# Two trunk layers on one core: the opening stage without GpSimd, its loads reordered, and some low parts in the FFNs issued earlier

## The chip, the core and the metric

The kernel runs on one core of a Trainium2 chip. A core has TensorE (PE, matrix products), VectorE (DVE), ScalarE (ACT), GpSimd (POOL) and SyncE (SP), which here issues every DMA. The time is device microseconds (us) of one execution. The kernel before took a median of 1766.38 us in 3 runs (1763.32 to 1766.62).

## The reference

Two layers of a diffusion trunk work on 384 tokens (256 latent, 128 context) of width 1024. Per layer there are three sub-layers, each with its own modulation by a condition vector (one for latent, one for context tokens):

```
m = silu(cond) @ w_mod[l] + b_mod[l]             # 9 vectors of 1024: shift, scale, gate for 3 sub-layers
mod(x, i) = x * (1 + m[3i+1]) + m[3i]
h = (silu(mod(x,0) @ w1) * (mod(x,0) @ w3)) @ w2         # FFN, inner width 2816
x = LN(alpha * x + 0.5 * m[2] * h)
x = LN(alpha * x + m[5] * Mix(mod(x, 1)))                # three token mixers, gates, output projection
h = second FFN on mod(x, 2);  x = LN(alpha * x + 0.5 * m[8] * h)
```

All matrices are float32. So the kernel runs four FFNs and two mixers, and before the first product of the first FFN it needs the shift and scale of that sub-layer: 2048 columns of w_mod, 16 units of 128 columns, each times two conditions.

## The kernel before, in words

**Split products.** Each large product is made of three float32r products: a factor is split into a high part (its float32r rounding) and a low part (the rest), and hi*hi, hi*lo and lo*hi are added in PSUM (`mm3`). A unit of weights is a 128x1024 tile, 512 KB, loaded by SP (`raw`); ACT makes its high part (`whi`, L263) and DVE its low part (`wlo`, L268). `pump` splits units as long as fewer than ten are held, `take` hands the next one to PE, and `done` frees it.

**GEMVs.** All other modulation units (128 of them) are made while the FFNs and mixers run: a tile `wm` of w_mod is loaded, and DVE multiplies it with silu(cond), which stands broadcast on all partitions in `silu_bc`, and sums along the row: two passes per unit, one for each condition (`gemv_acc`, L312). In an FFN `tick` calls `pump` and then lets GEMVs run at a steady pace: `GEMV_TICKS` is the number of ticks over which the FFN's share (`FFN_GEMV`: 42 in the first) is spread. In the first FFN there are 52 ticks.

**FFN.** Chunk j is 128 of the 2816 inner columns. For it PE makes w1 and w3 products (PSUM tiles named `f`, 24 products of 128x384 each), ACT makes silu (`s`), DVE the product `h`, ACT its high part `hhi`, DVE its low part `hlo`. The low part is a function kept in the list `lows` and called after the next `tick`. One chunk later PE multiplies `hhi`, `hlo` with a unit of w2 into `acc`. The last six units of w2 are the `tail`: PE takes them one output tile after another, so that the last chunk's `hlo` is needed a few us after its `h`. In FFNs other than the first, chunks 0 and 1 are made first for latent tokens, then for context tokens in another layout (`f1c`, `hc`), which `ctx_h` transposes into place at chunk 2.

**Opening stage** (`start`). It loads x, the conditions, the 16 modulation units (`m`) and the first ten weight units (`w`), transposes x (`xr` to `xl`, `xc`), makes the modulation columns `AB`, applies them (`y`), splits the result into `xT_hi` and `xT_lo` for eight 128-row blocks of the model width, and runs the first four chunks of FFN 1 (PSUM tiles named `st`, 192 products). The modulation units are shared out: those in `ON_PE` are GEMVs on PE (two moving columns), those in `ON_POOL` are multiplied on POOL and summed on ACT, the others go to DVE. The conditions come as one row each, are split, spread over the partitions by eight matmuls against ones (`sb`), and run through silu. Five of ten `wlo`, and the four `hlo`, are made on POOL. The order on every engine comes from a list scheduler (`Jobs.emit`), which takes each job's planned duration and dependences; loads keep the order of `START_LOADS`. It counts PSUM banks ("B") as a stock, and not the 34 SBUF tiles ("Q") of 4 KB per partition in which all weights live.

Of the kernel before, what the change touches and what calls it, by code (L numbers as in the profile page):

```python
# [11 lines left out]
F32 = mybir.dt.float32  # L12
# [6 lines left out]
P = 128  # L19
# [23 lines left out]
N_PE0 = 16  # L43
ON_PE = (0, 3, 7, 8, 10)
ON_POOL = (5, 9, 15)
LO_ON_V = (0, 1, 4, 5, 9)
AFTER = 2
START_LOADS = [('m', 0), ('m', 2), ('x', 2), ('b', 0), ('m', 9), ('x', 5), ('w', 0), ('x', 4), ('x', 0), ('m', 8),
               ('w', 1), ('m', 10), ('x', 3), ('w', 2), ('m', 1), ('m', 3), ('w', 3), ('m', 11), ('w', 4), ('x', 1),
               ('m', 12), ('m', 5), ('w', 5), ('m', 4), ('w', 6), ('m', 7), ('m', 14), ('w', 7), ('m', 6), ('w', 8),  # L50
               ('m', 13), ('w', 9), ('m', 15)]
LATENCY = 0.18, 1.8
# [8 lines left out]
RES_AT = 5  # L61
GEMV_TICKS = 52
FFN_GEMV = {(0, 0): 42, (0, 1): 36, (1, 0): 36, (1, 1): 8}
# [117 lines left out]
def trunk_kernel(ctx: ExitStack, tc: tile.TileContext, wst, wmod, wmod0, x_lat, x_ctx, cvec, cT,  # L181
# [408 lines left out]
    def ffn(l, f, ctx_part, gate_at):  # L590
# [22 lines left out]
        else:  # L613
# [30 lines left out]
            rel(*bb)  # L644
            rel(sg)
            tick()

# [12 lines left out]
        for j in range(j0, NF):  # L660
            bb = []
            for w in ("w1", "w3"):
                i, hi, lo = take(w, l, f, j)
                b = get("B", [P, T], F32, "f1")
                for kc in range(KC):
                    mm3(b, (hi[:, kc * P:(kc + 1) * P], lo[:, kc * P:(kc + 1) * P]), xt(kc, 0, T), kc == 0, kc == KC - 1)
                done(i)
                bb.append(b)
                if w == "w3":
                    new_h(j)  # L670
                    lows.append(glu(bb[0], bb[1], T, *hT[j]))
                    rel(*bb)
                tick()
                while lows:
                    lows.pop(0)()
                if j == 2 and w == "w1":
                    ctx_h()
            if not first and j == RES_AT:
# [663 lines left out]
    with tc.manual_schedule():  # L1342
        def start(new_h, hT):
# [5 lines left out]
            sT = cst.tile([P, KC, 2], F32, name="sT")  # L1349
            ones = get("S", [1, P], F32R, "ones")  # L1350
            V.memset(ones.bitcast(F32), 1.0)
            box = {}


            def load(key, src, t=None, dur=1.46):
                def f():
                    box[key] = get("Q", [P, 1024], F32, "ld") if t is None else t
                    nc.sync.dma_start(box[key], src)
                return add("D", dur, [], f)

            def load_raw():
                return add("D", 1.46, [], issue_dma)

            crow = [get("Q", [1, 2, 512], F32, "crow") for _ in range(2)]
            ld = {"cT": load("cT", cT, cTs, .3)}
            for cd in range(2):
                ld["c", cd] = load(("c", cd), cvec[cd:cd + 1, :], crow[cd], .2)
            ld["id"] = load("id", cident, ident, .2)
            for kind, n in START_LOADS:
                if kind == "m":  # L1370
                    ld["m", n] = load(("m", n), wmod0[n])
                elif kind == "w":
                    ld["w", n] = load_raw()
                elif kind == "x":
# [4 lines left out]
                    ld["x", n] = load(("x", n), src[:, sl], xa[ti][:, sl], .73)  # L1379
# [5 lines left out]
            spread = []  # L1385
            for cd in range(2):
                hi, lo = get("Q", [1, 2, 512], F32R, "chi"), get("Q", [1, 2, 512], F32R, "clo")
                jh = add("A", .95, [ld["c", cd]], lambda hi=hi, cd=cd: S.copy(hi, crow[cd]))
                jl = add("V", 1.14, [jh], lambda hi=hi, lo=lo, cd=cd:
                         V.tensor_tensor(lo, crow[cd], hi.bitcast(F32), ALU.subtract))  # L1390

                def bc(cd=cd, parts=(hi, lo)):
                    for h in range(2):
                        b = get("B", [P, 512], F32, "sb")
                        for e in range(2):
                            mm(b, ones, parts[e][:, h, :], e == 0, e == 1)
                        box["sb", cd, h] = b
                    rel(crow[cd], *parts)
                jm = add("P", 1.7, [jl], bc, need=["B", "B"])
                for h in range(2):  # L1400
                    def ev(cd=cd, h=h):
                        b = box["sb", cd, h]
                        S.activation(sbc[:, cd, h * 512:(h + 1) * 512], b, AF.Silu)
                        rel(b)
                    spread.append(add("A", .5, [jm], ev, free=["B"]))

# [4 lines left out]
            for ti in range(3):  # L1411
                for h in range(2):
# [9 lines left out]
                    xev[ti, h] = add("A", .5, [add("P", .8, [ld["x", 2 * ti + h], ld["id"]], tr, need=["B"])], ev, free=["B"])  # L1422

# [15 lines left out]
            for kc in range(KC):  # L1439
                deps = []  # L1440
                for u in (KC + kc, kc):
                    col = modcol[0][:, u // KC, :, kc]
                    if u in ON_PE:
                        def f(u=u):
# [4 lines left out]
                            rel(box["m", u])  # L1449
                        deps.append(add("P", 1.8, [ld["m", u], silu_cols], f))  # L1450
                    else:
                        pool = u in ON_POOL
                        for cd in range(2):
                            if pool:
                                def f(u=u, cd=cd):
                                    w = box["m", u]
                                    t = box["mt", u, cd] = get("Q", [P, 1024], F32, "wms") if cd == 0 else w
                                    G.tensor_tensor(t, w, sbc[:, cd, :], ALU.mult)

                                def f2(u=u, cd=cd):  # L1460
                                    S.activation(junk, box["mt", u, cd], AF.Copy,
                                                 accum_out=modcol[0][:, u // KC, cd, u % KC:u % KC + 1])
                                    rel(box["mt", u, cd])
                                d = add("G", 2.3, [ld["m", u]] + spread + deps[-1:] * cd, f)
                                deps.append(add("A", 1.1, [d], f2))
                            else:
                                def f(u=u, cd=cd):
                                    gemv_acc(0, u, box["m", u], (cd,))
                                    if cd:
                                        rel(box["m", u])  # L1470
                                deps.append(add("V", 1.16, [ld["m", u]] + spread + deps[-1:] * cd, f))
# [5 lines left out]
                jab = add("V", .26, deps + [ld["b"]], f)  # L1477

# [11 lines left out]
                jy = add("A", .9, [jab] + [xev[ti, kc // 4] for ti in range(3)], fy)  # L1490
                lo_x.append(add("V", .5, [add("A", .45, [jy], fhi)], flo))

# [3 lines left out]
            for i in range(n_un + AFTER):  # L1496
                jh = add("A", .95, [ld["w", i]] + lo_w[-1:], split_hi)
                eng = "V" if i in LO_ON_V else "G"
                lo_w.append(add(eng, 2.3 if eng == "G" else 1.14, [jh], lambda e=eng: split_lo(G if e == "G" else V)))
            count = {}  # L1500
# [10 lines left out]
            for g in range(n_un):  # L1511
                last[g] = []
                for kc in range(KC):
                    last[g].append(add("P", .49, [lo_x[kc], lo_w[g]] + ([last[g - 1][kc]] if g else []) + last[g][:1],
                                       lambda g=g, kc=kc: prod(g, kc), need=["B"] if kc == 0 and g < 6 else []))
            for j in range(N_ST):
# [12 lines left out]
                def f4(j=j):  # L1529
                    G.tensor_tensor(hT[j][1], box["h", j], hT[j][0].bitcast(F32), ALU.subtract)  # L1530
                    rel(box["s", j], box["h", j])
                d = add("A", .4, last[2 * j], f1)
                d = add("V", .5, [d] + last[2 * j + 1], f2)
                d = add("A", .45, [d], f3)
                add("G", 1., [d], f4)
            jobs.emit({"B": 6})
            rel(ones, *xl, xc, box["wide"], *[box["st", g] for g in range(6)])
            for dst, src in ((lncol, lnT), (pscale, pscaleT), (subln, sublnT), (namask_t, namask)):
# [125 lines left out]
```

## Time and profile before

| What | Value |
|---|---|
| median of 3 runs | 1766.38 us |
| profiled execution, its span | 1768.49 us, 1766.8 us |
| PE busy | 1726.4 us, 98% of the span |
| DVE, ACT, POOL busy | 1245.9, 751.3, 37.4 us |
| mean granted clock of PE | 0.992 |
| the chain that ended last | PE 91%, DVE 4%, DMA 2% |

The profile is one execution. PE is on the chain nearly always, so time is to be looked for where PE waits, or where its clock is at the lower of its two levels (1.2 GHz, shown as 0.5, against 2.4 GHz, shown as 1.0). A table of waits names for each engine what it waited for, the total, the number of times and the longest. A window row shows busy time per engine in a stretch, the granted clock, the share of DMA time and GB/s.

### The profile page before, as it was taken

To read this page: it belongs to the slowest core of one execution; us is meant where nothing else is said; L and a number is where in the kernel's file an instruction comes from. 1 tells how busy PE (TensorE), PEld (TensorE's weight loads), DVE (VectorE), ACT (ScalarE), POOL (GpSimd) and SP (SyncE) were. 2 spreads that over 40 slices of the span, in tenths; PEclk is the share of its full clock that TensorE was granted. 3 is DMA by queue.
4 is the path that set the end of the run, shared out by engine and by line. 5 is a ranking of instruction groups with operands and counts; after the bars stand their busy time and mean duration, and the time that the engine had idled before them with its cause. 6 is when DMAs were issued, how large, how long until landed. Compare 5 with 4: busy or idle time off the path is not lost.

```text
span 1766.8 us, 24383 instructions
## 1 busy us (share of the span) xinstructions
PE 1726.4 (98%) x9444; PEld 1621.3 (92%) x9444; DVE 1245.9 (71%) x2045; ACT 751.3 (43%) x1322; POOL 37.4 (2%) x21
## 2 busy tenths in 40 slices
PE   7899998999999999999999999999999999999997
PEld 7799998899999989999998999988999999999996
DVE  6698888568785788787677788764778657755334
ACT  5433333358653452323353232334875445333321
POOL 3400000000000000000000000000000000000000
PEclk9899999999999999999999999999999999999999
DMA  8386665142446256566436666523223543644320
GB/s 319 120 291 228 238 222 196 72 169 75 138 155 226 96 207 231 206 235 223 151 122 235 224 217 229 203 88 133 106 104 117 191 143 104 237 169 141 137 96 36
DMA packets 88071, 301.64 MB, mean 171 GB/s; under 512 B 11058, under 2 KB 13970, under 8 KB 87956
## 3 DMA queue, kind: packets, MB, share of 16 engines
q1 hardware_dynamic: 87956, 300.09, 47.9%
q8 instruction: 74, 1.21, 0.3%
q14 instruction: 41, 0.34, 0.1%
HBM read 296.86 MB, written 3.19 MB: 170 GB/s over the span
## 4 chain that ended last, share of the span: by engine, by line
PE 91%; DVE 4%; DMA 2%; ACT 1%; issue 1%; SPq 0%; DVEq 0%; ACTq 0%
PE f L220 36%; PE acc L220 24%; PE gt L220 11%; PE v L220 4%; PE pj L220 4%; DVE junk L312 2%; PE qb L220 2%; PE kb L220 2%; PE o L220 1%; PE ss L220 1%; PE st L220 1%; PE f1c L220 1%; PE qc L220 1%; PE kc L220 1%; DMA wm<-in_wmod 1%
## 5 line engine op out<-in xcount | busy, mean ns | idle before, releaser
L268 DVE TENSOR_TENSOR wlo<-raw,whi 128x1024 fp32r<-128x1024 f32 x379 | 456.8, 1222 | 166.7 <-ACT whi L263 166.0
L220 PE MATMUL f<-xT_hi,whi 128*128 128x384 f32 (+1 forms) x1344 | 445.3, 331 | 0.0
L220 PE MATMUL f<-xT_hi,wlo 128*128 128x384 f32 (+1 forms) x1344 | 444.9, 331 | 0.0
L220 PE MATMUL f<-xT_lo,whi 128*128 128x384 f32 (+1 forms) x1344 | 444.6, 331 | 0.0
L263 ACT CAST whi<-raw 128x1024 fp32r<-128x1024 f32 x384 | 384.8, 1047 | 23.3 <-DMA raw<-in_wst 11.7
L312 DVE CUSTOM_DVE_ANT_0 junk<-wm,silu_bc 128x1024 bf16<-128x1024 f32 x256 | 312.5, 1221 | 6.8 <-DMA wm<-in_wmod 2.5
L220 PE MATMUL acc<-whi,hlo 128*128 128x512 f32 x624 | 246.7, 395 | 8.6 <-DVE hlo L586 8.5
L220 PEld LDWEIGHTS f<-xT_hi,whi 128*128 128x128 f32 x1344 | 252.7, 188 | 2.4
L220 PEld LDWEIGHTS f<-xT_lo,whi 128*128 128x128 f32 x1344 | 252.7, 188 | 2.4
L220 PEld LDWEIGHTS f<-xT_hi,wlo 128*128 128x128 f32 x1344 | 252.6, 188 | 0.0
L220 PE MATMUL acc<-whi,hhi 128*128 128x512 f32 x624 | 245.7, 394 | 0.9 <-ACT hhi L582 0.9
L220 PE MATMUL acc<-wlo,hhi 128*128 128x512 f32 x624 | 245.6, 394 | 0.0
L582 ACT CAST hhi<-h 128x384 fp32r<-128x384 f32 (+1 forms) x84 | 42.5, 506 | 360.0 <-DVE h L581 360.0
L220 PEld LDWEIGHTS acc<-whi,hlo 128*128 128x128 f32 x624 | 118.1, 189 | 35.5 <-DVE hlo L586 10.7
L579 ACT ACTIVATE s<-f 128x384 f32<-128x384 f32 (+1 forms) x84 | 40.7, 484 | 242.9 <-PE f L220 242.9
L581 DVE TENSOR_TENSOR h<-s,f 128x384 f32<-128x384 f32 (+1 forms) x84 | 45.5, 542 | 137.3 <-PE f L220 128.3
L220 PEld LDWEIGHTS acc<-whi,hhi 128*128 128x128 f32 x624 | 118.4, 190 | 24.4 <-ACT hhi L582 1.4
L220 PEld LDWEIGHTS acc<-wlo,hhi 128*128 128x128 f32 x624 | 118.1, 189 | 23.2
L220 PE MATMUL gt<-xT_hi,whi 128*128 128x384 f32 x384 | 130.2, 339 | 0.6 <-ACT whi L263 0.6
L220 PE MATMUL gt<-xT_hi,wlo 128*128 128x384 f32 x384 | 129.3, 337 | 1.4 <-DVE wlo L268 1.4
L220 PE MATMUL gt<-xT_lo,whi 128*128 128x384 f32 x384 | 129.2, 336 | 0.0
L220 PEld LDWEIGHTS gt<-xT_hi,wlo 128*128 128x128 f32 x384 | 72.7, 189 | 2.0 <-DVE wlo L268 2.0
(230 smaller groups left out, 2127.6 us busy)
## 6 DMA issues: line engine op xcount, KB each, us to landing
raw<-in_wst SPq DMA_DIRECT2D x384, 512.0 KB, 4.2
wm<-in_wmod SPq DMA_DIRECT2D x128, 512.0 KB, 4.6
ld<-in_wmod SPq DMA_DIRECT2D x16, 512.0 KB, 9.5
gate<-gd SPq DMA_DIRECT2D x12, 512.0 KB, 4.1
lng<-in_lnrow SPq DMA_DIRECT2D x6, 512.0 KB, 3.8
lnb<-in_lnrow SPq DMA_DIRECT2D x6, 512.0 KB, 5.1
nab<-in_nabias SPq DMA_DIRECT2D x4, 512.0 KB, 6.0
out<-y SPq DMA_DIRECT2D x6, 256.0 KB, 2.0
```

Of the source, the lines that this page charges most:

```text
L220: PE.matmul(out, a, b, start=start, stop=stop)
L263: S.copy(ws[i][0], raws[i])
L268: eng.tensor_tensor(ws[i][1], raw, ws[i][0].bitcast(F32), ALU.subtract)
L312: V.tensor_tensor_reduce(out=junk, in0=t, in1=silu_bc["t"][:, cd, :], scale=1.0, scalar=0.0, op0=ALU.mult, op1=ALU.add, accum_out=modcol[l ...
L579: S.activation(s, b1, AF.Silu)
L581: V.tensor_tensor(h, s, b3, ALU.mult)
L582: S.copy(hT_hi, h)
```

## The change

In the opening stage POOL has no work any more: the units of `ON_POOL`, the five `wlo` and the four `hlo` go to DVE, and the set of units on PE is another one, with six units for five. The two conditions are loaded broadcast to all partitions (512 KB each) straight into `silu_bc`, where ACT applies silu in place; the split, the matmuls against ones and their evacuations are gone. The loads stand in another order. The scheduler's durations are changed and it counts the "Q" tiles as a stock. In the FFNs the first two chunks' low parts are issued before the first `tick`, `ctx_h` before the `tick` of its place, and in the last chunk no GEMV is issued between `h` and `hlo`, and `pump` comes after them; `GEMV_TICKS` is 48 for 52.

```
-ON_PE = (0, 3, 7, 8, 10)
-ON_POOL = (5, 9, 15)
-LO_ON_V = (0, 1, 4, 5, 9)
+ON_PE = (1, 5, 7, 12, 13, 15)
-START_LOADS = [('m', 0), ('m', 2), ('x', 2), ('b', 0), ('m', 9), ('x', 5), ('w', 0), ('x', 4), ('x', 0), ('m', 8),
...
+START_LOADS = [('x', 2), ('x', 0), ('m', 0), ('m', 1), ('m', 9), ('m', 12), ('m', 8), ('x', 3), ('m', 7), ('b', 0),
+               ('m', 6), ('m', 10), ('x', 4), ('m', 15), ('x', 5), ('m', 2), ('m', 5), ('w', 0), ('w', 1), ('x', 1),
...
-GEMV_TICKS = 52
+GEMV_TICKS = 48
@@ ffn, after the context part of chunks 0 and 1
             rel(sg)
+            while lows:
+                lows.pop(0)()
             tick()
@@ ffn, in the loop over chunks
                     lows.append(glu(bb[0], bb[1], T, *hT[j]))
                     rel(*bb)
-                tick()
+                if j == 2 and w == "w1":
+                    ctx_h()
+                if j < NF - 1:
+                    tick()
                 while lows:
                     lows.pop(0)()
-                if j == 2 and w == "w1":
-                    ctx_h()
+                if j == NF - 1:
+                    pump()
@@ start
-            crow = [get("Q", [1, 2, 512], F32, "crow") for _ in range(2)]
-            ld = {"cT": load("cT", cT, cTs, .3)}
+            ld = {"cT": load("cT", cT, cTs, .1)}
             for cd in range(2):
-                ld["c", cd] = load(("c", cd), cvec[cd:cd + 1, :], crow[cd], .2)
+                ld["c", cd] = load(("c", cd), cvec[cd:cd + 1, :].to_broadcast([P, DM]), sbc[:, cd, :], 1.3)
...
+            spread = [add("A", 1.15, [ld["c", cd]], lambda cd=cd: S.activation(sbc[:, cd, :], sbc[:, cd, :], AF.Silu))
+                      for cd in range(2)]
...
-                        deps.append(add("P", 1.8, [ld["m", u], silu_cols], f))
+                        deps.append(add("P", 3.15, [ld["m", u], silu_cols], f, free="Q"))
...
-                eng = "V" if i in LO_ON_V else "G"
-                lo_w.append(add(eng, 2.3 if eng == "G" else 1.14, [jh], lambda e=eng: split_lo(G if e == "G" else V)))
+                lo_w.append(add("V", 1.25, [jh], lambda: split_lo(V), free="Q"))
...
-                    G.tensor_tensor(hT[j][1], box["h", j], hT[j][0].bitcast(F32), ALU.subtract)
+                    V.tensor_tensor(hT[j][1], box["h", j], hT[j][0].bitcast(F32), ALU.subtract)
...
-            jobs.emit({"B": 6})
+            jobs.emit({"B": 6, "Q": len(free["Q"])})
```

On PE, at the start of the opening stage, before (the rows with sT are GEMV units, sb the broadcast, xr transposes of x, xT_hi the first wide products):

```order
L220 MATMUL st_116<-sT,ld_107 128x2 x8
L220 MATMUL sb_129<-chi_96,ones_89 128x512
...
L1416 MATMUL xr_148<-ident,xa_93 128x128 x4
L1416 MATMUL xr_156<-ident,xa_94 128x128 x4
L1416 MATMUL xr_168<-ident,xa_94 128x128 x4
L1416 MATMUL xr_176<-ident,xa_95 128x128 x4
L220 MATMUL st_116<-sT,ld_154 128x2 x8
L220 MATMUL st_116<-sT,ld_184 128x2 x8
L1416 MATMUL xr_223<-ident,xa_93 128x128 x4
L220 MATMUL st_235<-xT_hi,whi_162 128x384
```

The same place on PE now:

```order
L1397 MATMUL xr_106<-ident,xa_89 128x128 x4
L1397 MATMUL xr_113<-ident,xa_90 128x128 x4
L218 MATMUL st_125<-sT,ld_111 128x2 x8
L218 MATMUL st_125<-sT,ld_123 128x2 x8
L218 MATMUL st_125<-sT,ld_140 128x2 x8
L1397 MATMUL xr_177<-ident,xa_91 128x128 x4
L1397 MATMUL xr_183<-ident,xa_89 128x128 x4
L218 MATMUL st_125<-sT,ld_171 128x2 x8
L218 MATMUL st_125<-sT,ld_189 128x2 x8
L1397 MATMUL xr_241<-ident,xa_90 128x128 x4
L1397 MATMUL xr_252<-ident,xa_91 128x128 x4
L218 MATMUL st_259<-xT_hi,whi_224 128x384
```

Five of the GEMV units now stand ahead of the first wide product, where three did; the sixth follows six wide products later.

On DVE, at the end of the first FFN, from the last but one chunk's hlo, before (rows with junk are GEMV passes, r is the tail's first operation):

```order
L586 TENSOR_TENSOR hlo_2415<-h_2418,hhi_2414 128x384
L268 TENSOR_TENSOR wlo_2459<-raw_2383,whi_2458 128x1024
L312 ISA junk,modcol_72<-wm_2430,silu_bc 128x1024
...
L581 TENSOR_TENSOR h_2497<-s_2495,f_436_2468 128x384
L268 TENSOR_TENSOR wlo_2501<-raw_2425,whi_2500 128x1024
L312 ISA junk,modcol_72<-wm_2466,silu_bc 128x1024
L312 ISA modcol_72 128x1
L312 ISA junk,modcol_72<-wm_2466,silu_bc 128x1024
L312 ISA modcol_72 128x1
L586 TENSOR_TENSOR hlo_2494<-h_2497,hhi_2493 128x384
```

The same place now:

```order
L266 TENSOR_TENSOR wlo_2366<-raw_2293,whi_2365 128x1024
L579 TENSOR_TENSOR h_2400<-s_2398,f_410_2371 128x384
L266 TENSOR_TENSOR wlo_2404<-raw_2335,whi_2403 128x1024
L584 TENSOR_TENSOR hlo_2397<-h_2400,hhi_2396 128x384
L266 TENSOR_TENSOR wlo_2436<-raw_2369,whi_2435 128x1024
L579 TENSOR_TENSOR h_2470<-s_2468,f_422_2441 128x384
L584 TENSOR_TENSOR hlo_2467<-h_2470,hhi_2466 128x384
L266 TENSOR_TENSOR wlo_2475<-raw_2407,whi_2474 128x1024
```

The last two chunks have no GEMV pass any more, and the last hlo follows its h.

On DVE, at the start of the second FFN of layer 0, before (f1c is the context part of chunks 0 and 1, hcT its transposes):

```order
L643 TENSOR_TENSOR h_5964<-s_5962,f1c_5937 128x256
L268 TENSOR_TENSOR wlo_5967<-raw_5874,whi_5966 128x1024
...
L268 TENSOR_TENSOR wlo_6016<-raw_5982,whi_6015 128x1024
L312 ISA junk,modcol_72<-wm_6021,silu_bc 128x1024
L312 ISA modcol_72 128x1
L312 ISA junk,modcol_72<-wm_6021,silu_bc 128x1024
L312 ISA modcol_72 128x1
L586 TENSOR_TENSOR hlo_5752<-h_5805,hhi_5751 128x256
L586 TENSOR_TENSOR hlo_5809<-h_5909,hhi_5808 128x256
L654 TENSOR_TENSOR hlo_5752<-hcT_6029,hhi_5751 128x128
L654 TENSOR_TENSOR hlo_5809<-hcT_6029,hhi_5808 128x128
```

The same place now:

```order
L641 TENSOR_TENSOR h_5935<-s_5933,f1c_5908 128x256
L584 TENSOR_TENSOR hlo_5723<-h_5776,hhi_5722 128x256
L584 TENSOR_TENSOR hlo_5780<-h_5880,hhi_5779 128x256
L266 TENSOR_TENSOR wlo_5940<-raw_5845,whi_5939 128x1024
...
L654 TENSOR_TENSOR hlo_5723<-hcT_5988,hhi_5722 128x128
L654 TENSOR_TENSOR hlo_5780<-hcT_5988,hhi_5779 128x128
L266 TENSOR_TENSOR wlo_5996<-raw_5955,whi_5995 128x1024
L310 ISA junk,modcol_72<-wm_6001,silu_bc 128x1024
```

All four low parts moved ahead of the first GEMV, two of them ahead of every split.

## Rows read from the trace of the kernel before

**Rows 1.** Waits of PE, whole span: engine line waited for: total, times, longest

```profile
PE acc L220 <- DVE hlo L586: 8.5, 3, 4.4
PE st L220 <- DMA ld<-in_wmod: 6.3, 1, 6.3
PE st L220 <- DVE xT_lo L1488: 5.6, 3, 3.0
PE st L220 <- ACT xT_hi L1485: 4.0, 2, 3.7
...
PE acc L220 <- ACT hhi L582: 0.9, 1, 0.9
```

**Rows 2.** Windows: PE, PEld, DVE, ACT, POOL busy, PEclk, DMA share, GB/s

```profile
20.00:30.00 10.00, 9.56 (x43) 9.47 (x43) 7.66 (x15) 7.47 (x14) 2.46 (x1) 1.00 1.03 406
...
60.00:70.00 10.00, 3.25 (x11) 2.52 (x10) 8.41 (x12) 3.97 (x8) 5.90 (x2) 0.65 0.16 52
70.00:80.00 10.00, 9.45 (x43) 8.62 (x42) 2.06 (x4) 3.67 (x7) 0.00 (x0) 0.84 0.15 53
```

**Rows 3.** Groups of instructions, 0 to 110 us: busy, mean ns | idle before

```profile
L312 DVE CUSTOM_DVE_ANT_0 junk<-ld,silu_bc 128x1024 bf16<-128x1024 f32 x16 | 34.2, 2139 | 7.9 <-ACT silu_bc L1403 6.5 <-ACT junk L1461 1.2
```

**Rows 4.** The page's costliest groups, whole span

```profile
L268 DVE TENSOR_TENSOR wlo<-raw,whi 128x1024 fp32r<-128x1024 f32 x379 | 456.8, 1222 | 166.7 <-ACT whi L263 166.0
...
L312 DVE CUSTOM_DVE_ANT_0 junk<-wm,silu_bc 128x1024 bf16<-128x1024 f32 x256 | 312.5, 1221 | 6.8 <-DMA wm<-in_wmod 2.5
```

**Rows 5.** Timeline of DVE and POOL in the opening: start, us, instruction

```profile
62.56 1.21 DVE L312 CUSTOM_DVE_ANT_0 junk<-ld,silu_bc 128x1024 bf16<-128x1024 f32 x1
62.57 3.41 POOL L1458 TENSOR_TENSOR ld<-ld,silu_bc 128x1024 f32<-128x1024 f32 x1
...
63.81 3.25 DVE L312 CUSTOM_DVE_ANT_0 junk<-ld,silu_bc 128x1024 bf16<-128x1024 f32 x1
```

**Rows 6.** The chain that ended last, 0 to 130 us: start, us, what

```profile
2.24 3.93 DMA ld<-in_wmod
...
84.49 8.32 PE f L220 x48
```

**Rows 7.** Timeline of PE in the opening

```profile
6.31 3.54 PE L220 MATMUL st<-sT,ld 128*128 128x2 f32 x16 [6.31 <-DMA ld<-in_wmod]
...
13.48 3.67 PE L1416 MATMUL xr<-ident,xa 128*128 128x128 f32 x16
...
31.10 0.52 PE L220 MATMUL st<-xT_hi,wlo 128*128 128x384 f32 x1
31.42 0.52 PE L220 MATMUL st<-xT_hi,whi 128*128 128x384 f32 x1
...
35.93 0.34 PE L220 MATMUL st<-xT_hi,whi 128*128 128x384 f32 x1
```

**Rows 8.** The page's DMA issues: KB each, median us to landing

```profile
raw<-in_wst SPq DMA_DIRECT2D x384, 512.0 KB, 4.2
...
gate<-gd SPq DMA_DIRECT2D x12, 512.0 KB, 4.1
```

**Rows 9.** Timeline of PE at the end of the first FFN

```profile
309.94 0.80 PE L220 MATMUL acc<-whi,hlo 128*128 128x512 f32 x1 [4.35 <-DVE hlo L586]
```

**Rows 10.** Windows after two of the waits, columns as in rows 2

```profile
308.00:316.00 8.00, 6.06 (x15) 4.81 (x16) 2.20 (x8) 0.00 (x0) 0.00 (x0) 0.57 0.19 68
936.00:941.00 5.00, 5.00 (x16) 3.98 (x15) 3.11 (x4) 3.98 (x6) 0.00 (x0) 0.66 0.25 89
```

**Rows 11.** Timelines of DVE and PE at two FFN starts

```profile
651.91 1.22 DVE L312 CUSTOM_DVE_ANT_0 junk<-wm,silu_bc 128x1024 bf16<-128x1024 f32 x1 [0.82 <-DMA wm<-in_wmod]
...
654.80 0.50 PE L220 MATMUL acc<-whi,hlo 128*128 128x512 f32 x1 [1.64 <-DVE hlo L586]
...
935.45 0.50 PE L220 MATMUL acc<-whi,hlo 128*128 128x512 f32 x1 [2.52 <-DVE hlo L586]
```

**Rows 12.** Waits of DVE, 90 to 304 us

```profile
DVE wlo L268 <- ACT whi L263: 26.0, 17, 1.5
```

More of the change, by code (lines that the diff above doesn't have):

```diff
@@ L43 @@
 N_PE0 = 16
-ON_PE = (0, 3, 7, 8, 10)
-ON_POOL = (5, 9, 15)
-LO_ON_V = (0, 1, 4, 5, 9)
+ON_PE = (1, 5, 7, 12, 13, 15)
 AFTER = 2
-START_LOADS = [('m', 0), ('m', 2), ('x', 2), ('b', 0), ('m', 9), ('x', 5), ('w', 0), ('x', 4), ('x', 0), ('m', 8),
-               ('w', 1), ('m', 10), ('x', 3), ('w', 2), ('m', 1), ('m', 3), ('w', 3), ('m', 11), ('w', 4), ('x', 1),
-               ('m', 12), ('m', 5), ('w', 5), ('m', 4), ('w', 6), ('m', 7), ('m', 14), ('w', 7), ('m', 6), ('w', 8),
-               ('m', 13), ('w', 9), ('m', 15)]
+START_LOADS = [('x', 2), ('x', 0), ('m', 0), ('m', 1), ('m', 9), ('m', 12), ('m', 8), ('x', 3), ('m', 7), ('b', 0),
+               ('m', 6), ('m', 10), ('x', 4), ('m', 15), ('x', 5), ('m', 2), ('m', 5), ('w', 0), ('w', 1), ('x', 1),
+               ('m', 4), ('m', 13), ('w', 2), ('w', 3), ('w', 4), ('m', 11), ('w', 5), ('w', 6), ('w', 7), ('w', 8),
+               ('m', 14), ('w', 9), ('m', 3)]
 LATENCY = 0.18, 1.8
@@ L1349, in start, with load @@
             sT = cst.tile([P, KC, 2], F32, name="sT")
-            ones = get("S", [1, P], F32R, "ones")
-            V.memset(ones.bitcast(F32), 1.0)
             box = {}
-            def load(key, src, t=None, dur=1.46):
+            def load(key, src, t=None, dur=1.3):
                 def f():
@@ L1358, in f @@
                     nc.sync.dma_start(box[key], src)
-                return add("D", dur, [], f)
+                return add("D", dur, [], f, need="Q" * (t is None))
             def load_raw():
-                return add("D", 1.46, [], issue_dma)
-            crow = [get("Q", [1, 2, 512], F32, "crow") for _ in range(2)]
-            ld = {"cT": load("cT", cT, cTs, .3)}
+                return add("D", 1.3, [], issue_dma, need="Q")
+            ld = {"cT": load("cT", cT, cTs, .1)}
             for cd in range(2):
-                ld["c", cd] = load(("c", cd), cvec[cd:cd + 1, :], crow[cd], .2)
+                ld["c", cd] = load(("c", cd), cvec[cd:cd + 1, :].to_broadcast([P, DM]), sbc[:, cd, :], 1.3)
             ld["id"] = load("id", cident, ident, .2)
@@ L1378, in start @@
                     src = x_ctx[0] if ti == 2 else x_lat[0, ti * P:(ti + 1) * P, :]
-                    ld["x", n] = load(("x", n), src[:, sl], xa[ti][:, sl], .73)
+                    ld["x", n] = load(("x", n), src[:, sl], xa[ti][:, sl], .65)
                 else:
@@ L1384, in start @@
             silu_cols = add("A", .2, [ld["cT"]], lambda: S.activation(sT, cTs, AF.Silu))
[L1385 to L1405, printed above, removed]
+            spread = [add("A", 1.15, [ld["c", cd]], lambda cd=cd: S.activation(sbc[:, cd, :], sbc[:, cd, :], AF.Silu))
+                      for cd in range(2)]
             xl = [get("Q", [P, 4, 256], F32, "xl") for _ in range(2)]
@@ L1421, in ev @@
                         rel(b)
-                    xev[ti, h] = add("A", .5, [add("P", .8, [ld["x", 2 * ti + h], ld["id"]], tr, need=["B"])], ev, free=["B"])
+                    xev[ti, h] = add("A", .6, [add("P", .8, [ld["x", 2 * ti + h], ld["id"]], tr, need=["B"])], ev, free=["B"])
             def wide():
@@ L1449, in f @@
                             rel(box["m", u])
-                        deps.append(add("P", 1.8, [ld["m", u], silu_cols], f))
+                        deps.append(add("P", 3.15, [ld["m", u], silu_cols], f, free="Q"))
                     else:
-                        pool = u in ON_POOL
                         for cd in range(2):
[L1454 to L1471, printed above, removed]
+                            def f(u=u, cd=cd):
+                                gemv_acc(0, u, box["m", u], (cd,))
+                                if cd:
+                                    rel(box["m", u])
+                            deps.append(add("V", 1.3, [ld["m", u], spread[cd]] + deps[-1:] * cd, f, free="Q" * cd))
                 def f(kc=kc):
@@ L1476, in f @@
                                         bmod[:, 0, u:u + 1], float(1 - e), ALU.add, ALU.add)
-                jab = add("V", .26, deps + [ld["b"]], f)
+                jab = add("V", .4, deps + [ld["b"]], f)
                 def fy(kc=kc):
@@ L1489, in flo @@
                     rel(box["y", kc])
-                jy = add("A", .9, [jab] + [xev[ti, kc // 4] for ti in range(3)], fy)
-                lo_x.append(add("V", .5, [add("A", .45, [jy], fhi)], flo))
+                jy = add("A", 1.05, [jab] + [xev[ti, kc // 4] for ti in range(3)], fy)
+                lo_x.append(add("V", .56, [add("A", .5, [jy], fhi)], flo))
             n_un = 2 * N_ST
@@ L1496, in start @@
             for i in range(n_un + AFTER):
-                jh = add("A", .95, [ld["w", i]] + lo_w[-1:], split_hi)
-                eng = "V" if i in LO_ON_V else "G"
-                lo_w.append(add(eng, 2.3 if eng == "G" else 1.14, [jh], lambda e=eng: split_lo(G if e == "G" else V)))
+                jh = add("A", 1.05, [ld["w", i]] + lo_w[-1:], split_hi, need="QQ")
+                lo_w.append(add("V", 1.25, [jh], lambda: split_lo(V), free="Q"))
             count = {}
@@ L1513, in start @@
                 for kc in range(KC):
-                    last[g].append(add("P", .49, [lo_x[kc], lo_w[g]] + ([last[g - 1][kc]] if g else []) + last[g][:1],
-                                       lambda g=g, kc=kc: prod(g, kc), need=["B"] if kc == 0 and g < 6 else []))
+                    last[g].append(add("P", .52, [lo_x[kc], lo_w[g]] + ([last[g - 1][kc]] if g else []) + last[g][:1],
+                                       lambda g=g, kc=kc: prod(g, kc), need="B" if kc == 0 and g < 6 else "",
+                                       free="QQ" if kc == KC - 1 else ""))
             for j in range(N_ST):
@@ L1529, in f4 @@
                 def f4(j=j):
-                    G.tensor_tensor(hT[j][1], box["h", j], hT[j][0].bitcast(F32), ALU.subtract)
+                    V.tensor_tensor(hT[j][1], box["h", j], hT[j][0].bitcast(F32), ALU.subtract)
                     rel(box["s", j], box["h", j])
[L1532 to L1535, printed above, removed]
-            jobs.emit({"B": 6})
-            rel(ones, *xl, xc, box["wide"], *[box["st", g] for g in range(6)])
+                d = add("A", .5, last[2 * j], f1)
+                d = add("V", .55, [d] + last[2 * j + 1], f2)
+                d = add("A", .5, [d], f3)
+                add("V", .55, [d], f4)
+            jobs.emit({"B": 6, "Q": len(free["Q"])})
+            rel(*xl, xc, box["wide"], *[box["st", g] for g in range(6)])
             for dst, src in ((lncol, lnT), (pscale, pscaleT), (subln, sublnT), (namask_t, namask)):
```

## The prediction, made before the changed kernel ran

> **What bounds the kernel now.** I read the table of waits for TensorE over the whole span first, because TensorE (PE) is busy 98% of it: only where it waits, or runs at the lower of its two clocks, is there time to win. It waits 8.5 us for DVE's hlo and then, in the opening stage, 6.3, 5.6 and 4.0 us for the first load, for xT_lo and for xT_hi [rows 1]; the other rows of that table are 1.4 us or less. So the bound is PE's own work nearly everywhere, and the change can act in two places: the opening stage, up to the first product named f at 84.49 us [rows 6], and the few gaps at either end of the FFNs.
>
> Second, the opening in windows [rows 2]. The loads run at 406 GB/s early on, but from 60 to 70 us PE is busy 3.25 of 10 us with a granted clock of 0.65, and 0.84 in the next window, while the loads rest (a DMA share of 0.16). Third, what DVE does there: its sixteen GEMV passes take 2139 ns each [rows 3], against 1221 ns in the rest of the kernel [rows 4]. The timeline shows why: a pass that starts at 62.56, just ahead of a GpSimd (POOL) multiply, takes 1.21 us; the next starts at 63.81, beside that multiply of 3.41 us, and takes 3.25 us [rows 5]. So DVE is slowed by POOL, PE waits for DVE's columns, and the clock falls while PE waits.
>
> The Trainium skill (SBUF — State Buffer, section on the two separate sides) calls the port that DVE and GpSimd share an exclusive lock: the loser stands still until the holder's instruction is over. By it a pass behind a multiply of 3.41 us takes up to 4.6 us (an estimate from rows 4 and 5), where the row shows 3.25; sixteen such passes would be 74 us and not the measured 34.2. Neither enters the sum below, since no POOL work is left in the stage.
>
> **The change, part by part.** *Opening stage.* Added up for after, PE's own queue sets its end, so I walk along that queue.
>
> Start. In before the first 512 KB load is issued at 2.24 and is there 3.93 us later [rows 6]; after that 512 KB come every 1.29 us (0.524 MB at 406 GB/s, rows 2). Now two 512 KB broadcasts of the conditions, issued from about 1.2 us, stand ahead of everything but cT. The first lands at about 5.1, the second at 6.4, ident and two half tiles of x by 7.9, m0 (for DVE) at 9.2, m1 (PE's first GEMV unit) at 10.5. The broadcasts' cost is the unknown: the trace has 12 broadcast loads of the same size, the gates, with 4.1 us to landing against 4.2 for plain ones [rows 8], so nothing extra; at worst half as long again each, 1.3 us in all.
>
> PE's queue from 10.5: three GEMV units of 3.5 us, eight transposes, two units, eight transposes. A unit at the low clock is 3.54 us (its 16 records), a transpose 3.67/16 = 0.23 us [rows 7]. That is 5 x 3.5 + 16 x 0.23 = 21.2 us, to 31.7. By then w0 has landed: ten 512 KB loads, three half tiles and bmod after m1, 15 us, so 25.5, and its two splits take 2.3 us more. DVE is there too: twelve GEMV passes at 1.25 us, the spacing of 62.56 and 63.81 in rows 5, from 9.2 on end at 24.2, and the first xT columns under 2 us later.
>
> Wide products (128x384) then run at 0.32 us each (31.42 less 31.10 in rows 7) until the clock rises. In before that came at about 35.7, 5.4 us after the products became unbroken at 30.3 [rows 7], although PE had been busy with GEMV units and transposes since 6.3 (the clock column reads 1.00 so early, yet the products stand 0.32 us apart, and 0.17 later: I go by the products). In after: six wide products (1.9 us, to 33.6), the sixth GEMV unit (3.4, to 37.0), then 5.4 us at the low clock (17 products, to 42.4). The other 169 of 192 go at 8.32/48 = 0.173 us [rows 6]: 29.3 us, to 71.7. With some 0.5 us of small waits the opening ends at **72 us**, 12.5 earlier.
>
> A second way to the same number, from before's side: 84.5, less 9.6 us of waits for xT and some 2 of smaller ones, less 5.1 for the lower clock (0.35 and 0.16 of two 10 us windows, rows 2), plus 4.2 for the later start, plus 3.4 for the sixth GEMV unit, less 3.6 for the eight broadcast matmuls that go (9.85 to 13.48, rows 7), gives 71.8.
>
> What hides the rest: DVE takes over all of POOL's work. Its list up to the last xT_lo is 20 GEMV passes (25 us), seven splits of weights (8.6 at 1222 ns, rows 4) and eight xT_lo with sixteen AB (under 8): from 9.2 to about 51, at most 52 with its own waits. From the first product that needs the last two xT columns PE has 75 products left, 13 us; so DVE may be up to 58 before it costs anything. The last load (m3) is the 16 MB mark, 40 us of transfer, landed by 45; DVE gets to it then. If this cover of 6 us is gone, each further us costs one. Bounds for the opening: 69 (the clock rises at 37, the sixth unit is no break) and 77 (broadcasts slow, DVE 4 us over its cover).
>
> *Tail of the first FFN.* Before, the last chunk's hlo stands behind a weight split and two GEMV passes; PE waits 4.35 us for it [rows 9], plus 0.9 just ahead for the same chunk's hhi [rows 1], and then runs at the low clock: the window of 8 us from 308 has a granted clock of 0.57 [rows 10], 3.4 us lost. After, no GEMV is left in the last two chunks (48 ticks are used up by chunk 19) and h, hlo follow each other directly. All 8.7 us (4.35 + 0.9 + 3.4) go.
>
> What comes late instead: the 3.2 GEMVs that before has in those chunks (four ticks at 42/52; 8 us at two passes of 1.25) move into chunks 4 to 19, where DVE had 26.0 us of idle over 214 us, all of it spent waiting for ACT's whi [rows 12]. That is room on average, but in chunks 17 to 19 there is no w2 unit and only 8.3 us of PE per chunk, against two splits, h, hlo and 3.5 GEMV passes of DVE, 7.9 us, with splits for the tail's units on top. Then h is late and PE waits for a free bank. Bounds 0 and 8 us; no row shows such a wait in before, so I take the middle, **4 us**, each piece too short to pull the clock (1.64 us of idle at 654.80 did not [rows 11], 2.52 at 935.45 did). Net here 4.7.
>
> *Starts of the other FFNs.* In two of three the first chunks' hlo stand behind five splits and a GEMV whose weights land late (DVE idle to 651.91); PE waits 1.64 and 2.52 us [rows 11], and after the second the clock is 0.66 over 5 us [rows 10], 1.7 us. With hlo issued at once, before the splits, all 5.9 us go. What stands late next is the context part of hlo, which now precedes that GEMV too, and PE reaches it only after the first 12 products of that unit: no new wait. It can at worst take 1 us back at each start. The last chunk's order in the other FFNs moves nothing PE waits for: 0.
>
> Sum: 12.5 + 4.7 + 5.9 = 23.1. The profiled execution took 1768.49 us; 1745.4 follows. The median of the runs is 1766.38, 2.1 lower (they spread over 3.3), so the forecast for the median is **1744 us**.
>
> **Rivals.**
> A. *The first FFN keeps what it had.* The denser GEMVs make PE wait some 8 us for banks, one or two of these long enough to drop the clock. For it: DVE is over 80% busy there. Against: 26 us of idle. The term of 4.7 becomes 0 or slightly less: 1749 to 1752.
> B. *The clock stays low through the opening.* PE now has 10 us fewer of other work to cover, but more small matmuls and GEMV units in front. If the 186 wide products after the break all run at 0.32 us, the opening ends at 37 + 59.5 = 96.5, 12 later than before, and with 10.6 from the FFNs the result is 1768, no change. Against: in before the clock rose after 5.4 us of the same products.
> C. *Slower: DVE's long passes are not POOL's doing.* The place is DVE's queue in the opening, where loads run at full rate beside it. If every pass stays at 3.25 us, 20 passes are 65 us, with splits and columns slowed likewise some 95 us, so the last xT_lo is there at 104 and the stage ends at 117: +32, less 10.6: 1788. It decides from where DVE's list exceeds about 73 us (9.2 + 73 + 13 = 84.5 + 10.6). Against: the 1.21 us of the pass at 62.56, between two long ones.
> D. *The half of it:* passes stay at the mean of 2.14 us; 20 x 2.2 + 8.6 + 12 = 65 us, stage end 87, result 1759.
> E. *The loads of hlo were not what PE waited for* (the change does not do what it says in the FFNs): only the opening's 12.5 remains, 1754.
>
> **How the numbers follow.** Forecast 0.68 (its own range 1738 to 1749), A 0.14, E 0.06, D 0.04, B 0.05, C 0.03. Differences within 0.2% (3.5 us) are what a measurement of this kernel can't tell from none. Forecast, A, E and D lie below 1762.8: 0.92 faster; B is the same, 0.05; C slower, 0.03. The range that holds 8 in 10: down to 1735 (opening at 69, no new waits: 15.5 + 8.7 + 5.9 = 30), up to 1755, which takes in A and E.
>
> **What would show it.** In the profile after: DVE's GEMV passes in the opening at 1.22 us; the first product f at 72, unbroken products from about 37, the granted clock at its upper level from 42 and no fall before 300; no wait for hlo in TensorE's table; new short waits of f for DVE's h in the first FFN, 4 us in all. I am wrong if the first f comes after 78, if PE waits for xT_lo after 45, or if the waits of f for h pass 8 us.

## The result, and the profile after

The changed kernel took a median of 1738.25 us (4 runs, 1737.38 to 1740.61) against 1764.85 us for the kernel before in the same session (4 runs, 1763.09 to 1766.62): a ratio of 0.9851, 95% interval 0.9834 to 0.9868, so 26.6 us faster. The forecast was 1744 us; 1738.25 lies at the lower edge of its own range (1738 to 1749).

Waits of PE in the changed kernel, whole span (engine, line, what it waited for: total, times, longest), to set beside [rows 1]:

```profile
PE xr L1397 <- DMA xa<-in_x_lat: 8.0, 1, 8.0
PE gt L218 <- DVE wlo L266: 1.4, 1, 1.4
PE st L218 <- DMA ld<-in_wmod: 1.3, 1, 1.3
...
PE st L218 <- ACT s L1487: 0.6, 1, 0.6
...
PE f L218 <- DVE h L579: 0.4, 1, 0.4
```

The hlo row (8.5 us) and both xT rows (5.6 and 4.0) are gone. The new first row is the wait for the loads that now stand behind the broadcasts. The only new wait in the FFNs is 0.4 us of f for h.

DVE's GEMV passes in the opening, 0 to 110 us (count | busy, mean ns | idle before), to set beside [rows 3]:

```profile
L310 DVE CUSTOM_DVE_ANT_0 junk<-ld,silu_bc 128x1024 bf16<-128x1024 f32 x20 | 24.5, 1225 | 9.6 <-DMA ld<-in_wmod 9.1
```

Twenty passes take 24.5 us where sixteen took 34.2. PE's timeline in the opening (start, us, instruction), to set beside [rows 7]:

```profile
11.22 10.37 PE L218 MATMUL st<-sT,ld 128*128 128x2 f32 x48 [1.28 <-DMA ld<-in_wmod]
21.45 1.95 PE L1397 MATMUL xr<-ident,xa 128*128 128x128 f32 x8
23.20 6.83 PE L218 MATMUL st<-sT,ld 128*128 128x2 f32 x32
...
31.48 0.67 PE L218 MATMUL st<-xT_hi,whi 128*128 128x384 f32 x1
...
33.23 0.52 PE L218 MATMUL st<-xT_hi,wlo 128*128 128x384 f32 x1
33.55 1.99 PE L218 MATMUL st<-sT,ld 128*128 128x2 f32 x16
35.40 0.42 PE L218 MATMUL st<-xT_hi,whi 128*128 128x384 f32 x1
...
35.83 0.34 PE L218 MATMUL st<-xT_hi,wlo 128*128 128x384 f32 x1
36.01 0.33 PE L218 MATMUL st<-xT_hi,whi 128*128 128x384 f32 x1
```

The first five units run at 3.4 to 3.5 us each, the sixth takes 1.99: the clock rose inside it. From then on products start 0.17 us apart instead of 0.32. The chain that ended last, start, us, what [rows 6]:

```profile
38.03 0.47 DVE xT_lo L1455
...
38.54 26.11 PE st L218 x149
...
65.22 3.91 PE st L218 x21
69.13 8.32 PE f L218 x48
```

And windows of the changed kernel over the tail of the first FFN and the later of the two FFN starts that had waits, where they stand now (us, PE, PEld, DVE, ACT, POOL, PEclk, DMA share, GB/s) [rows 10]:

```profile
288.00:296.00 8.00, 8.00 (x37) 6.63 (x36) 3.44 (x8) 1.50 (x3) 0.00 (x0) 1.00 0.20 68
908.00:913.00 5.00, 5.00 (x24) 4.12 (x23) 3.43 (x7) 2.97 (x4) 0.00 (x0) 1.00 0.69 247
```

Full clock and no idle PE in either, where before had 0.57 and 0.66. The profiled execution took 1737.38 us, 31.1 less than the one of before (1768.49, itself 3.6 over its median). First f came 84.49 - 69.13 = 15.4 us earlier; the other 15.7 lie behind it.

### The profile page after: what moved, and what is told of

It reads as the page before. It is cut to its first block, busy times and chain, and to the rows that moved or that the text cites. A ratio compares the mean times of both kernels' runs of the same rounds, so it can differ in the third digit from the quotient of the medians.

```text
span 1735.5 us, 24394 instructions
## 1 busy us (share of the span) xinstructions
PE 1712.2 (99%) x9452; PEld 1613.5 (93%) x9452; DVE 1233.2 (71%) x2059; ACT 743.4 (43%) x1306; POOL 0.8 (0%) x6
## 3 DMA queue, kind: packets, MB, share of 16 engines
q8 instruction: 74, 1.21, 0.3%
## 4 chain that ended last, share of the span: by engine, by line
PE 91%; DVE 4%; issue 2%; ACT 1%; DMA 1%; SPq 0%; DVEq 0%; ACTq 0%
PE f L218 35%; PE acc L218 23%; PE gt L218 11%; PE v L218 4%; PE pj L218 4%; PE st L218 3%; PE qb L218 2%; PE kb L218 2%; DVE junk L310 2%; PE o L218 1%; PE ss L218 1%; DVE wlo L266 1%; PE f1c L218 1%; PE qc L218 1%; PE kc L218 1%
## 5 line engine op out<-in xcount | busy, mean ns | idle before, releaser
L266 DVE TENSOR_TENSOR wlo<-raw,whi 128x1024 fp32r<-128x1024 f32 x384 | 463.0, 1221 | 158.2 <-ACT whi L261 158.0
```

Of the source, the lines that this page charges most:

```text
L266: eng.tensor_tensor(ws[i][1], raw, ws[i][0].bitcast(F32), ALU.subtract)
```

## The experiments

All are compared with the kernel before, run beside them (medians 1765.2 to 1766.0 us).

**One half each.** `e1_open_only` has the new opening with the FFN code of before:

```
-GEMV_TICKS = 48
+GEMV_TICKS = 52
...
-            while lows:
-                lows.pop(0)()
             tick()
...
+                tick()
+                while lows:
+                    lows.pop(0)()
                 if j == 2 and w == "w1":
                     ctx_h()
-                if j < NF - 1:
-                    tick()
...
```

> The new opening stage with the FFN code and the pace of before (52 ticks). If the two parts add up, the opening keeps its 15.4 us (first f at 69.1 us) and the FFNs lose what the changed trace won at the hlo waits and their slow clock, 14.1 us (4.35 + 0.93 + 3.4 + 1.64 + 2.52 + 1.7 - 0.44): 1752 us, with PE waits for hlo of 8 to 9 us in the table again. Rival (the FFN edits move nothing, and the lost waits came with the shifted opening): 1738 to 1742 us, no hlo wait.

`e2_ffn_only` is the opposite: the opening of before, these FFN edits.

> The old opening stage with the FFN edits and 48 ticks. If the parts add up: 1764.9 - 14.1 = 1751 us, first f at 84.5, no PE wait for hlo. Rival (the FFN edits move nothing by themselves): 1762 to 1766 us, hlo waits of 8 us still there.

Measured: 1753.54 us (ratio 0.9933, 0.9921 to 0.9946) and 1753.58 us (0.9935, 0.9922 to 0.9947), first f at 68.78 and 84.16. Each half is worth 11.6 us by itself; both rivals fall. In the first, PE at the end of the first FFN:

```profile
289.26 0.50 PE L218 MATMUL acc<-whi,hhi 128*128 128x512 f32 x1 [1.04 <-ACT hhi L580]
...
294.35 0.79 PE L218 MATMUL acc<-whi,hlo 128*128 128x512 f32 x1 [4.36 <-DVE hlo L584]
```

These are the old waits, and the clock over the 8 us from 293 is 0.57 again. The halves add to 23.2, not to 26.6: both kernels came out 1.5 to 2.6 us slower than I expected from the profiled execution of before, which was slower than its median. Some 3 us of the medians' sum stay unassigned. Between profiled executions the halves do add, nearly: 1768.49 - 1753.54 = 14.95 and 1768.49 - 1753.58 = 14.91, against 31.11 for both. The 1.25 left is less than the 1.7 us of slow clock in the second mixer, which e1 and e2 have as before had it and the changed kernel has not (end of the next section).

**Which FFN edit.** `e4_ticks52` puts back the pace alone, `e5_last_chunk` the order of the last chunk alone, `e6_starts` the first chunks' low parts alone:

```
e4:  -GEMV_TICKS = 48
     +GEMV_TICKS = 52
e5:  -                if j < NF - 1:
     -                    tick()
     +                tick()
     ...
     -                if j == NF - 1:
     -                    pump()
e6:  -            while lows:
     -                lows.pop(0)()
                  tick()
```

> The changed kernel with GEMV_TICKS back at 52, all orders as changed. If the order in the last chunk alone took the tail's wait away: no hlo wait over 1 us at the end of the first FFN, 1737 to 1741 us. Rival (the pace did it): 4.35 + 0.9 us of waits and 3.4 us of slow clock come back there, 1747 us.

> The changed kernel (48 ticks) with only the last chunk's order undone: the tick stands again ahead of the low part. By the theory that the GEMVs between h and hlo made PE wait, it is enough that 48 ticks leave no GEMV there; only a weight split of 1.2 us stands in between: an hlo wait of 0 to 1 us at the end of the first FFN, 1737 to 1741 us. Rival (the order is what counts, the split alone holds hlo up): a wait of 2 to 4 us with the slow clock behind it, 1742 to 1746 us.

> The changed kernel with only the first chunks' low parts put back behind the tick. If these were what PE waited for at the other FFNs' starts: hlo waits of 1.6 and 2.5 us there again, and 1.7 us for each that the clock answers with a fall: 4.2 to 7.6 us more, 1742.5 to 1746 us. Rival (ctx_h ahead of the tick alone removes the waits): no hlo wait, 1737 to 1740 us.

Measured: 1737.85 us (0.9850, 0.9836 to 0.9863), 1741.85 us (0.9860, 0.9847 to 0.9874) and 1747.43 us (0.9888, 0.9874 to 0.9903). In e4 and e5 PE has no wait for hlo. So either edit removes the tail's wait, only both undone bring it back (e1). e5 lies 0.85 us above its expected range, e6 1.4. The 4 us between e4 and e5 are not explained by a wait: PE's waits differ by 0.45 us of f for h in e5, and the profiled executions by 2.0 (1737.80 and 1739.82). That more of e5's runs than of e4's had the later of the opening's two times (next section) could make up the rest, but this isn't shown: the one execution of each that was profiled had the earlier. In e6 two rows tell it, the wait and the window behind its first piece:

```profile
PE acc L218 <- DVE hlo L584: 4.6, 2, 2.3
```

```profile
635.00:640.00 5.00, 4.53 (x13) 3.59 (x14) 3.48 (x7) 3.36 (x4) 0.00 (x0) 0.66 0.63 206
```

That is 4.6 + 1.7 us (0.34 of 5 us), inside the expected 4.2 to 7.6. The rest of its 9.2 us over the changed kernel comes from its opening: first f at 72.25, see below. The two waits are equally long, 2.30 us before 635.47 and before 917.16, and only behind the first did the clock fall (1.00 from 917 to 921 us): the length of a wait does not settle it.

**GpSimd.** `e3_pool_busy` gives GpSimd work that nobody needs; `e7_tile_only` has its tile and none of its work; `e10_shift1024` a smaller tile:

```
+            scr = cst.tile([P, 480], F32, name="scr")     # e10: [P, 256]
+            G.memset(scr, 1.0)
+            for _ in range(32):                           # e3 only
+                G.tensor_tensor(scr, scr, scr, ALU.mult)  # e3 only
```

> The changed kernel with 32 multiplies of 128x480 on GpSimd from the start of the opening stage, on a tile of their own that nothing else reads (added work; nothing is left out). By the row of 128x384 in the trace before (1013 ns) they last some 40 us. If DVE's long passes were GpSimd's doing, passes beside them take 2 to 3 us instead of 1.22, DVE falls 12 to 20 us behind, and with its cover of some 5 us gone the first f comes at 76 to 85 us: 1745 to 1754 us. Rival (the passes were long for the loads or something else of the old stage): passes stay at 1.22 to 1.3 us, first f at 69, 1738 us.

> The changed kernel with the tile of the GpSimd test (1920 bytes per partition, one memset) but none of its multiplies, so the opening stage is as changed (first f at 69). In the GpSimd test products stood 175 ns apart instead of 173 through the whole kernel, some 10 us that no wait explains. If the moved addresses of all other tiles did that: 175 ns here too, 1746 to 1750 us. Rival (GpSimd's work or its aftermath did): 173 ns, 1738 us.

> The changed kernel with an unused tile of 1024 bytes per partition ahead of the weight tiles, where the tile of 1920 bytes made products of 128x384 stand 175 ns apart. If any shift of the weights against xT does that: 175 ns, 1747 to 1750 us. Rival (only some distances do): 173 ns, 1737 to 1741 us.

Measured: 1760.99 us (0.9972, 0.9963 to 0.9982), 1748.80 us (0.9903, 0.9889 to 0.9916) and 1739.85 us (0.9853, 0.9839 to 0.9868). DVE's passes in e3, 0 to 120 us, two of them in DVE's timeline, and what PE waits for:

```profile
L310 DVE CUSTOM_DVE_ANT_0 junk<-ld,silu_bc 128x1024 bf16<-128x1024 f32 x20 | 34.0, 1698 | 9.6 <-DMA ld<-in_wmod 9.1
```

```profile
23.50 1.21 DVE L310 CUSTOM_DVE_ANT_0 junk<-ld,silu_bc 128x1024 bf16<-128x1024 f32 x1
...
24.75 1.88 DVE L310 CUSTOM_DVE_ANT_0 junk<-ld,silu_bc 128x1024 bf16<-128x1024 f32 x1
```

```profile
PE st L218 <- DVE xT_lo L1459: 4.9, 3, 4.0
```

GpSimd alone makes the passes long again and brings PE's wait for xT_lo back; first f is at 81.50, in the expected 76 to 85. Against e7, GpSimd's work costs 1760.99 - 1748.80 = 12.2 us; between the profiled executions 8.6 of it lie in the opening (first f at 81.50 and 72.89). That the total is above the expected 1754 is the tile's doing, not GpSimd's (last section).

GpSimd's multiplies in e3: the eight before DVE's first pass, and the one beside the two passes above:

```profile
L1354 POOL TENSOR_TENSOR scr<-scr 128x480 f32<-128x480 f32 x8 | 7.9, 987 | 0.6
```

```profile
23.52 2.04 POOL L1354 TENSOR_TENSOR scr<-scr 128x480 f32<-128x480 f32 x1
```

The Trainium skill (SBUF — State Buffer, section on the two separate sides) has the loser of the shared port stand still until the holder is done. The trace agrees, both ways. The pass from 23.50 came first and took its 1.21 us; the multiply from 23.52 took 2.04 instead of 0.99; the next pass, from 24.75, ended 1.07 us after that multiply (26.63 and 25.56). So a pass is longer by about what is left of the multiply when it starts (0.66 us for 0.81 here), not by a whole multiply.

**GpSimd's part alone.** `e11_before_no_pool` is the kernel before with one edit of the opening: all of GpSimd's work on DVE.

```
-ON_POOL = (5, 9, 15)
-LO_ON_V = (0, 1, 4, 5, 9)
+ON_POOL = ()
+LO_ON_V = tuple(range(10))
...
-                    G.tensor_tensor(hT[j][1], box["h", j], hT[j][0].bitcast(F32), ALU.subtract)
+                    V.tensor_tensor(hT[j][1], box["h", j], hT[j][0].bitcast(F32), ALU.subtract)
...
-                add("G", 1., [d], f4)
+                add("V", .55, [d], f4)
```

> The kernel before, with only one part of the change: GpSimd's work in the opening stage goes to DVE (three units, five wlo, four hlo); units on PE, order of loads and spread of the conditions stay. If the freed port were all of the opening's gain: passes at 1.22 us, DVE's list from 12.5 us on (22 passes of 1.25, some eight splits, columns and low parts, 44 us, plus 3 us of its waits) ends at 60, first f at 73 to 76, 1754 to 1757 us. Rival (the load order and the units on PE are as much of it): passes are at 1.22 too, but in DVE's new list seven of the eight xT_lo stand behind the last pass, at 56 to 60 us; PE has some 168 of 192 products left then (29 us, and 3 to 5 at the slow clock): first f at 88 to 94, 1768 to 1775 us.

Measured: 1768.12 us (1.0010, 1.0001 to 1.0019), no gain, as the rival had it. Passes, last low parts, and the chain:

```profile
L312 DVE CUSTOM_DVE_ANT_0 junk<-ld,silu_bc 128x1024 bf16<-128x1024 f32 x22 | 26.9, 1223 | 6.8 <-ACT silu_bc L1403 6.3
```

```profile
54.85 3.36 DVE L1488 TENSOR_TENSOR xT_lo<-y,xT_hi 128x384 fp32r<-128x384 f32 x7
```

```profile
55.46 28.10 PE st L220 x149
...
88.06 7.11 PE f L220 x41
```

The passes are short, and yet first f comes at 88.06, later than the 84.49 of before: seven of eight xT_lo stand behind the last pass, and PE starts the last 170 of its 192 products only at 55.46 (149, and 21 behind a short wait for ACT). So DVE without GpSimd beside it is needed (e3) and not enough; its columns must also come out one by one. Which part of the rest brings that about, the units on PE, the order of the loads, the broadcast conditions or the scheduler's durations, was not tried one at a time.

**PE's part.** `e8_warm` adds wide products ahead of everything; `e9_five_pe` takes the sixth unit off PE:

```
e8:  +            V.memset(xT[0][:, 0, :].bitcast(F32), 1.0)
     +            dummy = get("B", [P, 512], F32, "dummy")
     +            for _ in range(24):
     +                mm(dummy[:, :T], xT[0][:, 0, 0:P], xT[0][:, 0, :], True, True)
     +            rel(dummy)
e9:  -ON_PE = (1, 5, 7, 12, 13, 15)
     +ON_PE = (1, 5, 7, 12, 15)
```

> The changed kernel with 24 products of 128x384 added on PE ahead of its first transposes (on ones, into a bank that nobody reads; nothing is left out), in the 8 us in which PE waits for the first loads. The step of the prediction that failed is when the clock rises: here it is asked of PE by itself. If unbroken wide products raise it wherever they stand, it is up after 2.4 to 5.4 us of them, the products go from 0.32 to 0.17 us apart; if it then stays up through transposes and GEMV units, five units take 1.8 us instead of 3.45, PE is 8 to 10 us ahead, and DVE's last xT_lo (53.6 in the changed trace) sets the end: first f at 65 to 67, 1734 to 1736 us. Rival (units of two columns don't hold the clock): units at 3.45 again, first f at 69 to 70, 1738 to 1739 us.

> The changed kernel with five GEMV units on PE instead of six: m13, the unit that breaks the wide products at 33.6, goes to DVE. PE loses 1.9 us of work (two wide products' place and 1.99 us of unit), DVE gains two passes, 2.5 us, so its last xT_lo moves from 53.6 to about 56. The prediction gave DVE a cover of 6 us; the changed trace leaves about 2 (the last 75 products and the last wait start at 55.6). If PE's queue sets the end with a cover of 6: first f at 67, 1736 us. If the cover is 2: DVE's end at 56 less PE's new need at 53.6, first f at 69.5 to 71, 1738.5 to 1740 us, with PE waits for xT of 2 us or more in the table.

Measured: e8 1737.02 us (0.9841, 0.9826 to 0.9855), no different from the changed kernel. PE's timeline:

```profile
1.35 6.00 PE L218 MATMUL dummy<-xT_hi 128*128 128x384 f32 x24 [1.35 <-DVE xT_hi L1351]
7.73 1.24 PE L1402 MATMUL xr<-ident,xa 128*128 128x128 f32 x8 [0.38 <-DMA xa<-in_x_lat]
10.99 9.84 PE L218 MATMUL st<-sT,ld 128*128 128x2 f32 x48 [2.02 <-DMA ld<-in_wmod]
20.68 1.95 PE L1402 MATMUL xr<-ident,xa 128*128 128x128 f32 x8
22.42 6.83 PE L218 MATMUL st<-sT,ld 128*128 128x2 f32 x32
```

The clock did rise (24 products in 6.00 us, eight transposes in 1.24 against 1.95), and fell at 11.6, after the 2.02 us of waiting; the units then took 3.4 us each as ever, and 20 us of them and of transposes did not raise it; it rose at 32.1, four wide products later. Whether units with no wait ahead of them would have kept it up was not tried.

e9 took 1746.70 us (0.9890, 0.9873 to 0.9906): slower than the changed kernel, and outside both expectations. Its table of waits:

```profile
PE st L218 <- DVE wlo L266: 6.9, 4, 2.8
```

With another set of units the scheduler wrote another list for DVE; five of eight xT_lo now end between 53.1 and 55.7 us, and PE runs dry four times before, each time for a wlo; first f is at 78.7. The clock is at its lower level from 48.6 to 55.4. My two expectations moved one end of a list and took its order as given.

## Why the prediction was right, and where it was off

- **The bound, and the opening's mechanism:** right in the main. Passes are at 1.225 us (1.22 forecast), with which rivals C and D fall. That GpSimd made them long is shown from both sides: long with its work alone added (e3), 1.223 us with its work alone taken from the stage of before (e11). The first wide product stood at 31.48 (31.7 forecast).
- **The port:** the 4.6 us set against 3.25 are no disagreement. The pass of 3.25 started at 63.81, 1.24 us into the multiply, and ended at 67.06, 1.08 after it [rows 5], as in e3. And only seven of before's sixteen passes took 3.2 us or more; the other nine took 1.2, so nothing called for 74.
- **PE's own queue as what sets the end:** it did from 38.5 us on, and not always before. In the changed kernel DVE's list is on the chain up to 38.54, where PE stood 0.27 us for an xT_lo; in e1 it is not. In e4 the clock rose 1.8 us earlier than in e1 (see the next point), and PE waited for DVE instead: from the first unit to first f it is 57.9 us in both.
- **The term that was mis-sized: "5.4 us more at the low clock", 42.4 for the rise, first f at 72.** It was 33.9 and 69.13, next to the lower bound of 69. The same opening in six other kernels, one profiled execution each, shows that both occur: the granted clock rose (the profile's first record of it; its column reads 1.00 ahead of that too) at 32.3 to 34.1 us in four (the changed kernel, e1, e4, e5; first f at 68.8 to 69.1) and at 41.7 to 42.0 in three (e6, e7, e10; first f at 72.3 to 72.9). In e10 the unit and products are as forecast:

```profile
33.57 3.41 PE L218 MATMUL st<-sT,ld 128*128 128x2 f32 x16
...
41.78 0.46 PE L218 MATMUL st<-xT_hi,whi 128*128 128x384 f32 x1
42.08 0.34 PE L218 MATMUL st<-xT_lo,whi 128*128 128x384 f32 x1
```

  PE's work up to there is the same in all seven. So the term has two values 3.4 us apart, and nothing in the kernels' edits says which; from one trace I had taken one. (The opening of before varies too: its trace has the rise at 35.7, and in e2 the clock was down again, at 0.50, from 21 to 27 us.) The Trainium skill (TensorE: Matmul & The Clock Gate, Part 1) says of such a warm-up that "it's run-variable", and these traces agree.
- **DVE's cover of 6 us:** too large. The last xT_lo ended at 53.65 (forecast 51, at most 52), and PE needed it at 69.13 less 75 x 0.173 and 0.54 of its last wait, 55.6: 2 us were left. It held at the end of the list, though not at 38.5 (above).
- **The start:** m1 was there at 11.22, 0.7 later than worked out; units and transposes took 20.3 us instead of 21.2, which made it good.
- **Tail of the first FFN:** 8.7 us gone as forecast, but the "4 us of new waits for banks" were 0.44. The mechanism was there: in the last chunk with GEMVs between its s and h, h starts 7.0 us after s.

```profile
265.53 0.48 ACT L577 ACTIVATE s<-f 128x384 f32<-128x384 f32 x1
```

```profile
272.49 0.55 DVE L579 TENSOR_TENSOR h<-s,f 128x384 f32<-128x384 f32 x1
```

```profile
273.09 0.44 PE L218 MATMUL f<-xT_hi,whi 128*128 128x384 f32 x1 [0.44 <-DVE h L579]
```

  That is the one wait of f. A chunk earlier h came 6.6 us after its s (256.04 and 262.63) and no f waited, so PE can do without h for about that long, and the passes end before more is asked. I had taken the middle of 0 and 8 without a row for it; rival A was this term at its worst, and it fell. Of my two reasons for the gain, pace and order, e4 and e5 show that either would have done.
- **"Too short to pull the clock":** the two rows with 1.64 and 2.52 us set no limit. In before the clock also fell behind waits of 0.62 and 1.38 us in the second mixer (0.57 from 1305 to 1309), and in e6 behind one of two waits of 2.30.
- **Starts of the other FFNs:** 5.9 forecast; e6 has 6.3 in its waits and clock. Right, and rival E falls with e2 and e6.
- **Rival B** (low clock throughout) had for it only that small matmuls don't raise the clock. In e8 20 us of them did not, but wide products did, at either of two times.
- The 23.1 us of the sum against 31.1 between the profiled executions: 15.4 against 12.5 in the opening, 3.6 in the new waits that did not come, and about 1.7 in the second mixer, where PE's waits of 0.6 and 1.4 us for gt are as before and the clock this time did not fall (in e4, with the same waits, it did: 0.79 over 8 us). The median gives back what before's execution had over its own. All three errors lean the same way, and the clock's part of them differs from one execution to the next, so that the median came out 0.25 us inside my own range is in part luck: the profiled execution lies 0.6 outside.

## What to carry to other kernels

Taking GpSimd off the stage paid only together with an order in which DVE's results come out piece by piece: moved alone, the same work gained nothing. Where either of two edits may have removed a wait, undo them one at a time and both at once, or the gain goes to the wrong one. And a term that rests on the instant at which TensorE's clock rises needs more than one execution: here it had two values, 3.4 us apart.

## What the runs showed of the hardware that was not expected

An unused tile of 1920 bytes per partition, which moves the weight tiles against xT, costs some 10 us over the whole kernel (e7, 1748.80 against 1738.25): the 48 products of the first f group take 8.45 us in place of 8.32.

```profile
72.89 8.45 PE f L218 x48
```

From start to start products of 128x384 stand 175 ns apart by the median over 100 to 1700 us, and 173 in the changed kernel, where there are 6152 of them; products of 128x512 keep 227. A tile of 1024 bytes (e10) does nothing of the kind:

```profile
72.57 8.32 PE f L218 x48
```

So where the operands lie counts. Whether it is their distance or the weight tiles' own address, and which values are bad, was not tried further. A kernel that adds a small tile can lose more by this than the tile's work costs.
